# A layer of two token mixers: norms between blocks placed later, and one half-weight's low part made on chip in place of stored and loaded

## The chip, the cores and the metric

The kernel runs on one core of a Trainium2 chip. The metric is the device time of one execution in microseconds, the median over runs. The output is float32, and every large product is made of three products of float32 halves (below).

## The reference

2112 tokens (a prompt of 2048 and a decode of 64) pass one layer of width 1024. All weights are dense matrices.

```python
def encoder_layer(x, p, conv_hist, S0, lb, w_in, conv_w, g_pre, g_onorm, w_a_out, w_b_out, w_o,
                  g_post, g_ple, w_ple_gate, w_ple_proj):
    h = rms_norm(x, g_pre)
    proj = jnp.einsum('btd,dn->btn', h, w_in)
    vA, bA, cA, zA, q, f, iv, zB, gA, gB = split_cols(proj)       # ten groups of 1024 columns
    u = cA * vA
    ...
    yA = jnp.einsum('btc,cd->btd', jax.nn.silu(zA) * bA * conv, w_a_out)
    ...
    fg = lb + (1.0 - lb) * jax.nn.sigmoid(f)
    ...
    S_new, o = hgrn2_scan(S0, qq, kk, vv, logf)                   # 8 heads of 128, chunks of 64
    o = o * lax.rsqrt(jnp.mean(o * o, axis=-1, keepdims=True) + EPS)
    yB = jnp.einsum('btc,cd->btd', o * jax.nn.silu(zB), w_b_out)
    merged = jax.nn.sigmoid(gA) * yA + jax.nn.sigmoid(gB) * yB
    out = jnp.einsum('btd,de->bte', merged, w_o)
    x = x + rms_norm(out, g_post)
    gate = jax.nn.sigmoid(jnp.einsum('btd,de->bte', rms_norm(x, g_ple), w_ple_gate))
    x = x + jnp.einsum('btp,pd->btd', p, w_ple_proj) * gate
```

## The kernel before

**Blocks.** The tokens go through the whole layer in three blocks of 768, 704 and 640, one after the other, features on the partitions. The state of the eight heads and the convolution's history are carried from block to block.

**Products.** A float32 operand is split in a high part `hi` (a copy to the type that TensorE multiplies, made by ScalarE) and a low part `lo` (the operand less `hi`, a subtract on VectorE): `split`, line 230 for both. A product is hi·hi + hi·lo + lo·hi, the matmuls of lines 459, 460 and 461 (the third multiplies the weight's `lo`). The big matrices are taken in pairs of column blocks `i1`, `i2` of 128, each with two halves of its 1024 rows, as 2x2 blocks A11, A12 (both of `i1`), A21, A22 (both of `i2`), and `sgroup` forms their product with seven block products instead of eight (`PRODUCTS`): four of them use sums of weight blocks (S1 to S4), the others A11, A12 and A22. A12 stands fifth. One product is 12 matmuls.

**Where a low part comes from.** In block 0 `combined` loads the weights, makes the sums and splits all; what is asked for later is stored: sums by `keep_sum` (`S<-s`, line 341) and low parts by `split_w` (`low<-lo`, line 288), both on the sync engine's queue SP. In blocks 1 and 2 `kept_w` loads a weight block (`raw`) and makes `hi`; its `lo` is either loaded from the store (`lo<-low`, line 282) or made again on chip (line 230). `used_later(idx, part)` decides in block 0 which low parts are stored, and `among(idx, part)` in `kept_w` which are made on chip. Part 1 is the second half of the rows: A12 for `i1`, A22 for `i2`. The ten groups of columns have the numbers VA, BA, CA, ZA, QQ, FF, IV, ZB, GA, GB from 0 to 9, of eight column blocks each. A head takes its F and Q columns as one pair (`i1` from FF, `i2` from QQ) and its Z and V columns as another (`i1` from ZB, `i2` from IV).

**Order.** Instructions are written by Python generators, and a scheduler that keeps to each engine's written order where it can, with buffers taken from pools (48 row buffers `r`, 4 `lo`, 5 `raw`, 3 `s`), sets the final order. After each product `sgroup` calls `hook()`, which takes the next entry from a list and runs it: so side work is put between products. `spread_out((gen, counts))` fills that list: the n-th number says how many steps of the generator are run after the n-th product from there. `placed` and `paced` bind an instruction or a DMA behind the last matmul written.

**Heads.** Per head `head_prep` makes f, q, k, v with their decays (a scan L986 and L988, exponentials L999 and L1000 on ScalarE, L1002 and L1003 on VectorE); k is turned to rows by tokens (L1072 on VectorE, two DMAs through DRAM, `tk<-r` and `r<-tk`, and a copy L1085 on GpSimd). `head_attn` has TensorE form each chunk's update (L1149), VectorE add it to the state in a chain (L1164, five of them one after the other in block 2), and TensorE multiply the scores (L1187) and the states before (L1189) into the output. Line 1226 scales the head's output, L479 and L488 take products out of the accumulators.

**Norms between blocks.** At the end of block 0 and of block 1, `final_norm` runs among the first gate products of the next block. Its steps: square sums (`sum_squares`, line 749), the first transposes on TensorE that turn the sums to columns (line 726), the root on GpSimd (706), the spread back over the columns by TensorE (714), then a step for each of eight features tiles, a second round of transposes and spread, and a step for each column tile that splits it for the gate (line 230). The x rows are stored and loaded on GpSimd's queue by the same steps. `final_gate` (matmuls of lines 648 to 650) follows after seven products.

Of the kernel before, what the change touches and what calls it, by code (L numbers as in the profile page):

```python
# [20 lines left out]
KB = D // P  # L21
# [10 lines left out]
VA, BA, CA, ZA, QQ, FF, IV, ZB, GA, GB = range(10)  # L32
# [62 lines left out]
def hybrid_step(  # L95
# [46 lines left out]
    def sized(bl, steps):  # L142

        while True:
            with sized_to(bl):
                try:
                    made = next(steps)
                except StopIteration:
                    return
            yield made  # L150
# [4 lines left out]
    def rt(n=0, dt=F32):  # L155
        t = ring.tile([P, BN + 2], dt, tag="r", name=nm("r"))
        return t if n is None else t[:, : n or width[0]]
# [80 lines left out]
    def load_raw(src):  # L238
        raw = wp.tile([P, 4, P], F32, tag="raw", name=nm("raw"), bufs=5)
        SP.dma_start(raw, src)  # L240
        return raw
# [13 lines left out]
    def used_later(idx, part):  # L255

        if idx // 8 in (QQ, IV) and part == 1:
            return False  # L260
        if GA * 8 <= idx < GB * 8 + KB - 2:
            return part in ("S1", "S2", "S3", "S4")
        if idx in (GB * 8 + KB - 1, IV * 8):
            return part != 0
        if idx < QQ * 8:
            return part != 1
        if W_B <= idx < W_O:
            return part == 1 and idx - W_B >= KH
        return True

    def split_w(raw, key=None, spread=False, among_sums=False):


        hi = wp.tile([P, 4, P], F32R, tag="hi", name=nm("hi"))
        if spread:
            lo = low_tile()
            split(raw, hi, lo)
            return hi, lo
        if key in lows:
            lo = wp.tile([P, 4, P], F32R, tag="lo", name=nm("lo")) if among_sums else low_tile()  # L280
            A.copy(hi, raw)  # L281
            SP.dma_start(lo.bitcast(F32), lows[key])
            return hi, lo
        lo = wp.tile([P, 4, P], F32R, tag="lo", name=nm("lo"))
        split(raw, hi, lo)
        if key is not None and used_later(*key):
            lows[key] = dram.tile([P, 4, P], F32, tag=f"lo{key}", name=nm("low"), bufs=1)
            stores[0].dma_start(lows[key], lo.bitcast(F32))
        return hi, lo
# [24 lines left out]
    def behind_all(marks):  # L314

        order = ExitStack()
        for ins in marks:
            order.enter_context(tc.issue_after(ins))
        return order
# [8 lines left out]
    def run(gen, n=None):  # L328
        for i, _ in enumerate(gen):
            if n is not None and i + 1 == n:  # L330
                break
# [12 lines left out]
    def kept_w(i1, i2, name, anew=False, spread=False):  # L344

        def among(idx, part):
            return part == 1 and (idx < QQ * 8 or idx // 8 in (QQ, IV))

        keys = dict(A11=(i1, 0), A12=(i1, 1), A22=(i2, 1))
        if name in keys:  # L350
            return split_w(load_raw(w_blk[keys[name]]), None if anew else keys[name], spread or among(*keys[name]))
        return split_w(load_raw(sums[i1][name]), (i1, name))
# [139 lines left out]
    def half(t, h):  # L492
        return t[:, h * hn() : (h + 1) * hn()]
# [58 lines left out]
    def narrow(src):  # L552
        one = rt(dt=F32R)
        split(src, half(one, 0), half(one, 1))
        return half(one, 0), half(one, 1)
# [979 lines left out]
    def spread_out(*plans):  # L1535


        def steps(todo):
            with behind_all(m for m in copies + adds if m is not None):
                for gen, n in todo:  # L1540
                    run(gen, n)

        for counts in zip_longest(*(plan for _, plan in plans), fillvalue=0):
            todo = [(gen, n) for (gen, _), n in zip(plans, counts) if n]
            hooks.append(partial(steps, todo) if todo else None)
# [131 lines left out]
    for bi, bl in enumerate(blocks):  # L1677
        first, kept = bi == 0, kepts[bi]
        width[0] = bl["n"]
        segs = bl["segs"]  # L1680
        if bi == 1:
            stores[0] = G
        ahead_of = (*range(W_A, W_A + KH), W_O, W_O + 1) if first else None if bl["last"] else range(W_B, W_B + KH)
        path_b(bl, hc, first, kept, fills, hs if first else None, ahead_of and prepare_sums(ahead_of, pieces=True))
        if not bl["last"]:
            run(fills)
        a = []
        nxt = None if bl["last"] else blocks[bi + 1]
        cols, a_first = [], []
        rows = sized(nxt, row_rstd(nxt, cols)) if nxt else iter(())  # L1690
        sums_ahead = prepare_sums((W_O + 2, W_O + 3), True) if first else iter(())

        def side(rows):
            for j in range(KB):
                if 1 <= j <= 5:
                    next(rows, None)
                if j == 2:
                    next(fills, None)
                yield

        def ready():
            a_first.extend(narrow(half(t, 0)) for t in a[:KH])

        path_a(bl, hc, a, first, side(rows), ready)
        assert not hooks
        mg, xo, h2, acc = [], [], [], rt()

        def next_ops():

            with sized_to(nxt):  # L1710
                made = sized(nxt, operands(hc, x_rs[0], partial(load_x, nxt)))
                next(made)
            return made

        def ask_rs():
            with sized_to(nxt):
                x_rs.append(broadcast(cols[0]))

        x_rs = []

        if nxt:
            hc = new_operands()
        stages = [out_in_turn(mg, xo, acc, bl["last"])]
        before, loads, ob, m = merge_in_turn(a, kept, mg, first)
        loads(W_A, -1)
        if first:
            for idx, n in in_turn(before, a_first):
                loads(idx, n)
            next(sums_ahead)
            a_first.clear()  # L1730
            for j, _ in enumerate(merge_plain(bl, ob, m, kept, mg, sums_ahead)):
                if j == KB - 4:
                    ask_rs()
                if j == KB - 2:
                    a_first.extend(narrow(half(t, 0)) for t in mg[:KH])
                    ops = next_ops()
            spread_out((ops, (0, 1, 0, 1, 0, 1, 0) * KH))
            loads = lambda idx, n: None
        else:
            stages = before + stages  # L1740
        if bl["last"]:
            ps = load_p(bl, G)
        for idx, n in in_turn(stages, a_first):
            loads(idx, n)
            if nxt and (idx, n) == (W_B, 4):
                ask_rs()
            elif nxt and (idx, n) == (W_B, 6):
                spread_out((next_ops(), (0, 1, 0, 1, 0, 1, 0) * KH))
            elif nxt:
                pass  # L1750
            elif (idx, n) == (W_B, 5):
                ph = [split_rt(raw) for raw in ps]
            elif (idx, n) == (W_O, 4):
                norms = [final_norm(bl, [s], xo, acc, h2, None, s is segs[1]) for s in segs]
                spread_out((norms[0], (1, 0, 1, 1, 1, 0, 1, 0)))
        if nxt:
            xo.extend(stages[-1]["mid"])
            fills = sized(nxt, gates(nxt, hc, kepts[bi + 1], False))
            norm = sized(bl, final_norm(bl, segs, xo, acc, h2, kept))
            spread_out((norm, (1, 1, 1, 1, 1, 1, 0, 1, 0, 0, 0, 0, 1, 1) + (0, 1) * (KB - 1) + (0, 0, 1, 0, 0, 1) + (0, 1) * (KB - 1) + (1,)))  # L1760
            run(fills, LEAD)
            assert not hooks
            run(final_gate(bl, segs, xo, h2, kept))
        else:

            gate = [final_gate(bl, [s], xo, h2, kept, anew=s is segs[1], held={} if s is segs[1] else {0: 0, 1: 0, 2: 0, 3: 2, 4: 0, 5: 4}) for s in segs]
            spread_out((norms[0], (2, 2, 1, 0, 1, 1, 4, 4)), (norms[1], (0,) * 6 + (1, 1) + (1, 1, 1, 0, 0, 1, 0, 1, 4, 4)))
            run(ple(bl, ph, kept, spare=range(KB)))
            run(gate[0], 2)
            with behind_all(copies[:1]):  # L1770
                run(norms[1], KB)
            run(gate[0])
            assert not hooks
            run(gate[1])
# [49 lines left out]
```

## Time and profile before

| | |
|---|---|
| median of 3 runs | 2522.61 us (2521.67 to 2523.67) |
| the profiled execution's own time | 2521.4 us |
| its span | 2519.7 us |
| granted TensorE clock | 1.0 |
| TensorE busy | 2500.6 us |
| VectorE busy | 1868.3 us |
| ScalarE busy | 1489.6 us |
| GpSimd busy | 480.7 us |
| DMA | 748.77 MB, mean 297 GB/s |
| loads `lo<-low` on SP | 387 of 256 KB |
| stores `low<-lo` on SP | 223 of 256 KB |

The span runs from the first to the last instruction of the profiled execution; the time of a run has some 1.7 us more around it. A busy share is the time in which an engine has an instruction under way. In a timeline a row begins with the start and the length of an instruction in us from the span's start; a bracket at its end is the engine's idle time ahead of it, and what ended it. `x24` is a count, 128x512 a tile of 128 partitions by 512 elements.

### The profile page before, as it was taken

The numbers are of one execution on the slowest core, as the hardware profiler recorded it, in microseconds if no ns is written. First come the engines' busy times: TensorE is split into PE (matmuls) and PEld (weight loads), VectorE is DVE, ScalarE is ACT, GpSimd is POOL, SyncE is SP. The second block draws the span as 40 slices with busy tenths as digits, with TensorE's granted clock in tenths as the row PEclk, the third lists the DMA queues.
The fourth block names the chain that finished last, engine by engine and source line by source line (L and its number), as shares of the span: only waits on it lengthen the run. The fifth ranks groups of instructions, "written<-read, shape, count | busy, mean of one in ns | idle before, by whom it ended". The sixth has DMA issues, their size and how long they took to land.

```text
span 2519.7 us, 47327 instructions
## 1 busy us (share of the span) xinstructions
PE 2500.6 (99%) x16302; PEld 2481.2 (98%) x16302; DVE 1868.3 (74%) x3607; ACT 1489.6 (59%) x2902; POOL 480.7 (19%) x819
## 2 busy tenths in 40 slices
PE   9999999999999999999999999999999999999999
PEld 9999999999999999999999999999999999999998
DVE  7888898988868775577785657987357776446967
ACT  6666676654453764466655556576456665545675
POOL 2032223221022021122223211102212221001111
PEclk9999999999999999999999999999999999999999
DMA  8788988997697798788889988979988997878985
GB/s 333 250 300 316 333 323 303 348 328 270 231 348 244 244 332 299 266 285 302 303 289 315 346 297 301 331 266 333 327 292 308 313 303 262 266 255 313 338 272 200
DMA packets 350961, 748.77 MB, mean 297 GB/s; under 512 B 43702, under 2 KB 49136, under 8 KB 350720
## 3 DMA queue, kind: packets, MB, share of 16 engines
q1 hardware_dynamic: 298944, 541.26, 62.3%
q0 software_dynamic: 51776, 204.48, 23.1%
q8 instruction: 128, 2.10, 0.3%
q14 instruction: 113, 0.93, 0.1%
HBM read 540.29 MB, written 205.28 MB: 296 GB/s over the span
## 4 chain that ended last, share of the span: by engine, by line
PE 88%; DVE 4%; DMA 3%; issue 3%; ACT 1%; POOL 0%; SPq 0%; DVEq 0%; ACTq 0%; POOLq 0%
PE pg L459 19%; PE pg L461 19%; PE pg L460 18%; PE pg L611 5%; PE pg L610 5%; PE pg L612 5%; PE pg L650 3%; PE pg L649 3%; PE pg L648 3%; DMA raw<-w_blk 1%; PE pa L1117 1%; PE pa L1187 1%; PE pa L1149 1%; PE pa L1189 1%; DVE lo L230 1%
## 5 line engine op out<-in xcount | busy, mean ns | idle before, releaser
L459 PE MATMUL pg<-r,hi 128*128 128x320 f32 (+2 forms) x3304 | 1074.9, 325 | 1.9 <-ACT hf L473 1.2
L460 PE MATMUL pg<-r,hi 128*128 128x320 f32 (+2 forms) x3304 | 1067.1, 323 | 0.0
L461 PE MATMUL pg<-r,lo 128*128 128x384 f32 (+2 forms) x2380 | 776.2, 326 | 3.3 <-DVE lo L230 3.0
L281 ACT CAST hi<-raw 128x512 fp32r<-128x512 f32 x626 | 386.4, 620 | 434.2 <-PE pg L460 188.9
L459 PEld LDWEIGHTS pg<-r,hi 128*128 128x128 f32 x3304 | 621.2, 188 | 4.7 <-ACT hf L473 1.9
L460 PEld LDWEIGHTS pg<-r,hi 128*128 128x128 f32 x3304 | 621.3, 188 | 0.0
L461 PEld LDWEIGHTS pg<-r,lo 128*128 128x128 f32 x2380 | 447.1, 188 | 5.4 <-DVE lo L230 4.2
L230 ACT CAST hi<-raw 128x512 fp32r<-128x512 f32 x348 | 215.6, 622 | 181.1 <-PE pg L460 48.2
L461 PE MATMUL pg<-r,s 128*128 128x352 f32 (+1 forms) x924 | 292.0, 316 | 0.0
L611 PE MATMUL pg<-r,hi 128*128 128x320 f32 (+2 forms) x864 | 277.6, 322 | 0.9 <-DVE r L230 0.8
L610 PE MATMUL pg<-r,hi 128*128 128x320 f32 (+2 forms) x864 | 274.9, 322 | 0.0
L230 DVE TENSOR_TENSOR r<-r,r 128x320 fp32r<-128x320 f32 (+7 forms) x350 | 206.4, 608 | 45.0 <-ACT r L230 43.2
L230 DVE TENSOR_TENSOR lo<-raw,hi 128x512 fp32r<-128x512 f32 x264 | 181.1, 689 | 76.6 <-ACT hi L230 71.7
L230 ACT CAST r<-r 128x320 fp32r<-128x320 f32 (+7 forms) x350 | 183.8, 556 | 45.8 <-DVE r L403 11.9
L612 PE MATMUL pg<-r,lo 128*128 128x352 f32 (+2 forms) x564 | 180.7, 321 | 0.0
L461 PEld LDWEIGHTS pg<-r,s 128*128 128x128 f32 x924 | 173.4, 188 | 0.0
L230 ACT CAST hi<-s 128x512 fp32r<-128x512 f32 x164 | 101.7, 623 | 115.4 <-PE pg L460 87.5
L649 PE MATMUL pg<-r,hi 128*128 128x384 f32 (+2 forms) x512 | 166.9, 327 | 0.2 <-DVE r L230 0.2
L648 PE MATMUL pg<-r,hi 128*128 128x384 f32 (+2 forms) x512 | 165.8, 327 | 0.2 <-ACT hi L281 0.2
L611 PEld LDWEIGHTS pg<-r,hi 128*128 128x128 f32 x864 | 162.1, 188 | 2.8 <-DVE r L230 2.2
L610 PEld LDWEIGHTS pg<-r,hi 128*128 128x128 f32 x864 | 161.3, 188 | 1.3 <-ACT r L230 0.7
L473 ACT COPY hf<-pg 128x352 f32<-128x352 f32 (+2 forms) x354 | 157.0, 447 | 1.1 <-PE pg L461 1.1
(383 smaller groups left out, 4155.3 us busy)
## 6 DMA issues: line engine op xcount, KB each, us to landing
raw<-w_blk SPq DMA_DIRECT2D x579, 256.0 KB, 4.4
raw<-S SPq DMA_DIRECT2D x436, 256.0 KB, 4.2
lo<-low SPq DMA_DIRECT2D x387, 256.0 KB, 4.3
s<-low SPq DMA_DIRECT2D x239, 256.0 KB, 4.5
low<-lo SPq DMA_DIRECT2D x223, 256.0 KB, 4.0
S<-s SPq DMA_DIRECT2D x152, 256.0 KB, 3.9
low<-r POOLq DMA_DIRECT2D x50, 256.0 KB, 4.7
r<-w_blk POOLq DMA_DIRECT2D x48, 256.0 KB, 6.6
```

Source lines behind the costliest of these rows:

```text
L230: return A.copy(hi, src).ins, V.tensor_tensor(lo, src, hi.bitcast(F32), ALU.subtract).ins
L281: A.copy(hi, raw)
L459: add(hi[:, k, :], xhi, start=start and k == 0, stop=False)
L460: add(hi[:, k, :], xlo, start=False, stop=False)
L461: last[0] = add(lo[:, k, :], xhi, start=False, stop=k == KH - 1).ins
L473: copied = A.copy(got[n], ps[bank])
L610: add(hi[:, k, :], xhi, start=start and k == 0, stop=False)
L611: add(hi[:, k, :], xlo, start=False, stop=False)
L612: last[0] = add(lo[:, k, :], xhi, start=False, stop=k == KH - 1).ins
L648: T.matmul(ps, hi[:, k % 4, :], xhi[:, c], start=k == ks[0], stop=False)
L649: T.matmul(ps, hi[:, k % 4, :], xlo[:, c], start=False, stop=False)
L650: last[0] = T.matmul(ps, lo[:, k % 4, :], xhi[:, c], start=False, stop=k == ks[-1]).ins
```

## The change

Two edits. The first: the second half-rows' low parts of the F and Z groups (A12 of both pairs of every head) are no longer stored in block 0 nor loaded in blocks 1 and 2, but made on chip by a subtract. The Q and V groups' A22 was already so; the A12 of the first four groups too. 16 stores and 32 loads go, 32 subtracts come. The second: the list of counts for the norms between blocks. Counted in products from 0, the first transposes move from 7 to 11, their spread from 12 to 14, the eight column steps from 13, 15, ... 27 to 15, 17, ... 29, the second transposes from 30 to 32, the second spread from 33 to 35, and the last steps from 35, 37, ... 47, 48 to 36, 38, 40, 42, 44, 46, 47, 48.

```diff
-        if idx // 8 in (QQ, IV) and part == 1:
-            return False
         if GA * 8 <= idx < GB * 8 + KB - 2:
             return part in ("S1", "S2", "S3", "S4")
         if idx in (GB * 8 + KB - 1, IV * 8):
-            return part != 0
-        if idx < QQ * 8:
+            return part != 0 and (part != 1 or idx >= GA * 8)
+        if idx < GA * 8:
             return part != 1
...
     def kept_w(i1, i2, name, anew=False, spread=False):
         def among(idx, part):
-            return part == 1 and (idx < QQ * 8 or idx // 8 in (QQ, IV))
+            return part == 1 and idx < GA * 8
...
-            spread_out((norm, (1, 1, 1, 1, 1, 1, 0, 1, 0, 0, 0, 0, 1, 1) + (0, 1) * (KB - 1) + (0, 0, 1, 0, 0, 1) + (0, 1) * (KB - 1) + (1,)))
+            spread_out((norm, (1,) * 6 + (0,) * 5 + (1, 0, 0, 1, 1) + (0, 1) * (KB - 1) + (0, 0, 1, 0, 0, 1) + (1, 0) * (KB - 3) + (1, 1, 1)))
```

The two removed lines stand at the top of `used_later`, so that from there on every line of the changed kernel has a number two lower: its L1162 is L1164 of before. The numbers behind tile names count up in the order of allocation.

The sync engine's queue in block 0, in the first heads, before: between two loads of weights stand a store of a sum (L341) and stores of low parts (L288).

```order
L341 DMA S_646_2709<-s_2707 128x512
L288 DMA low_2506<-lo_2503 128x512
L240 DMA raw_2699<-w_blk 128x512
L240 DMA raw_2930<-w_blk 128x512
L341 DMA S_651_2719<-s_2717 128x512
L288 DMA low_2512<-lo_2509 128x512
L240 DMA raw_2932<-w_blk 128x512
L288 DMA low_2526<-lo_2523 128x512
L341 DMA S_656_2729<-s_2727 128x512
```

The same place of that queue after the change (the stores of sums are L339, of low parts L286 there):

```order
L339 DMA S_639_2695<-s_2693 128x512
L286 DMA low_2494<-lo_2491 128x512
L240 DMA raw_2685<-w_blk 128x512
L240 DMA raw_2914<-w_blk 128x512
L339 DMA S_644_2705<-s_2703 128x512
L240 DMA raw_2916<-w_blk 128x512
L286 DMA low_2512<-lo_2509 128x512
L339 DMA S_649_2715<-s_2713 128x512
```

One of the two stores of low parts between the last two sums is gone (A12's); the rest of the order, and that of the other engines in block 0, is the same.

VectorE in a head of block 2, before: the scan (L986, L988), the five steps of the state's chain (L1164, the first with `state`, the last into `one`) and what stands between them.

```order
L986 SCALAR_TENSOR_TENSOR r_24350<-keep,r_24349 128x640
L1164 SCALAR_TENSOR_TENSOR r_24442<-state_14315,qc_23954,pa_24437 128x128
L988 TENSOR_TENSOR r_24349<-r_24350 128x640
L230 TENSOR_TENSOR s_24398<-raw_24395,hi_24397 128x512
L1164 SCALAR_TENSOR_TENSOR r_24442<-r_24442,qc_23954,pa_24437 128x128
L1226 TENSOR_TENSOR r_23555<-r_24103,r_23555 128x640
L1164 SCALAR_TENSOR_TENSOR r_24442<-r_24442,qc_23954,pa_24437 128x128
L1003 COPY qc_24360<-qc_24360 128x1
L488 TENSOR_TENSOR hf_24435<-hf_24435,hf_24467 128x320
L1164 SCALAR_TENSOR_TENSOR r_24442<-r_24442,qc_23954,pa_24437 128x128
L1002 TENSOR_TENSOR qc_24360<-qc_24360,r_24351 128x9
L479 TENSOR_TENSOR hf_24420<-hf_24420,pg_24486 128x320
```

The same head after the change, each line number two lower:

```order
L984 SCALAR_TENSOR_TENSOR r_24318<-keep,r_24317 128x640
L230 TENSOR_TENSOR lo_24360<-raw_24357,hi_24359 128x512
L230 TENSOR_TENSOR s_24366<-raw_24363,hi_24365 128x512
L986 TENSOR_TENSOR r_24317<-r_24318 128x640
L1162 SCALAR_TENSOR_TENSOR r_24410<-state_14283,qc_23922,pa_24405 128x128
L1224 TENSOR_TENSOR r_23523<-r_24071,r_23523 128x640
L1162 SCALAR_TENSOR_TENSOR r_24410<-r_24410,qc_23922,pa_24405 128x128
L1001 COPY qc_24328<-qc_24328 128x1
L1000 TENSOR_TENSOR qc_24328<-qc_24328,r_24319 128x9
L1162 SCALAR_TENSOR_TENSOR r_24410<-r_24410,qc_23922,pa_24405 128x128
L477 TENSOR_TENSOR hf_24388<-hf_24388,pg_24454 128x320
L1162 SCALAR_TENSOR_TENSOR r_24410<-r_24410,qc_23922,pa_24405 128x128
```

The new subtract (`lo` from `raw`) and the old one (into an `s` buffer) stand ahead of the chain's first step, and L1002 (L1000 there) ahead of its third.

TensorE where the norm between blocks 0 and 1 makes its first transposes (L726), before:

```order
L459 MATMUL pg_11193<-r_10855,hi_11120 128x352
L460 MATMUL pg_11193<-r_10856,hi_11120 128x352
L461 MATMUL pg_11193<-r_10855,lo_11121 128x352
L726 MATMUL pa_11164<-ident,r_8743 128x128 x3
L726 MATMUL pa_11169<-ident,r_8743 128x128 x3
L459 MATMUL pg_11148<-r_10323,hi_11132 128x352
```

And after the change:

```order
L457 MATMUL pg_11116<-r_10869,hi_11100 128x352
L458 MATMUL pg_11116<-r_10870,hi_11100 128x352
L459 MATMUL pg_11116<-r_10869,lo_11101 128x352
L724 MATMUL pa_11189<-ident,r_8711 128x128 x3
L724 MATMUL pa_11194<-ident,r_8711 128x128 x3
L457 MATMUL pg_11131<-r_10239,hi_11106 128x352
```

The product that came next before (`pg_11148`, called `pg_11116` after) and the one behind it now stand ahead of the transposes: they are 24 matmuls later. At the boundary of blocks 1 and 2 they are 16 matmuls later.

## The prediction

> **What bounds the kernel now.** I read the page first: the span, the share of each engine, the chain that ended last.
> ```profile
> span 2519.7 us, 47327 instructions
> PE 2500.6 (99%) x16302; PEld 2481.2 (98%) x16302; DVE 1868.3 (74%) x3607; ACT 1489.6 (59%) x2902; POOL 480.7 (19%) x819
> PE 88%; DVE 4%; DMA 3%; issue 3%; ACT 1%; POOL 0%; SPq 0%; DVEq 0%; ACTq 0%; POOLq 0%
> ```
> TensorE is busy for 99% of the span, and the chain is 88% TensorE. The change takes no matmul away, so it can only win or lose the gaps between matmuls. Next I asked for TensorE's waits in the stretches that the change touches: the heads of block 0 (100 to 460 us), the norms between blocks (870 to 960 and 1690 to 1790) and the heads of block 1 (1040 to 1330).
> ```profile
> PE pg L461 <- DVE lo L230: 3.0, 2, 1.7
> PE pg L459 <- ACT hf L473: 1.2, 2, 0.7
> PE pg L459 <- ACT hi L230: 0.6, 1, 0.6
> ...
> PE pa L726 <- DVE r L749: 1.2, 1, 1.2
> ...
> PE pa L726 <- DVE r L749: 1.4, 1, 1.4
> PE pa L714 <- POOL cols L706: 0.2, 1, 0.2
> ...
> PE pa L1149 <- POOL r L1085: 0.4, 1, 0.4
> ```
> The first three rows are block 0's: 4.8 us, and a fourth row of 0.2 us makes 5.0. The next three are the boundaries', the last is block 1's only one. The heads of block 2 (1790 to 2130) have no TensorE wait at all. So 5.0 + 2.8 + 0.4 us is nearly all that can be won there, and nothing hinders block 2 today: what the change adds there can only cost.
>
> The waits of VectorE over block 0's heads (100 to 460) say why TensorE waits for `lo`:
> ```profile
> DVE lo L230 <- DMA low<-lo: 19.8, 10, 4.4
> ```
> It stands still ten times until a store of a `lo` tile has landed, because the buffer that it wants to write is still being read by that store.
>
> **The change part by part.**
>
> *Stores that go (block 0).* 16 of the `low<-lo` stores go, those of A12 in the eight F and eight Z groups. The timeline shows one of them issued on the sync queue, three of the waits it is part of, and a TensorE stall soon after:
> ```profile
> 155.76 0.69 DVE L230 TENSOR_TENSOR lo<-s,hi 128x512 fp32r<-128x512 f32 x1 [3.29 <-DMA low<-lo]
> ...
> 199.74 1.97 SPq L288 DMA_DIRECT2D low<-lo  x1
> ...
> 208.75 0.69 DVE L230 TENSOR_TENSOR lo<-s,hi 128x512 fp32r<-128x512 f32 x1 [4.38 <-DMA low<-lo]
> ...
> 220.15 0.44 PE L461 MATMUL pg<-r,lo 128*128 128x384 f32 x1 [1.71 <-DVE lo L230]
> ...
> 408.20 0.69 DVE L230 TENSOR_TENSOR lo<-s,hi 128x512 fp32r<-128x512 f32 x1 [3.66 <-DMA low<-lo]
> ```
> The bracket is the idle time ahead of the instruction and what ended it. Matched with the program's order, the five longest of the ten waits (first and last quoted, the longest between) are all waits for A12's stores; they go, and that is most of the 19.8 us. TensorE's stall at 220.15 comes 11 us after VectorE was held for 4.38 us, with its split of the next weights late. If VectorE is no longer held, all 5.0 us of TensorE's idle time go: −5.0. The bounds are −6 (each of six stalls also refills the pipeline, about 0.16 us each) and −2 (the stores of sums that stay are next in the queue, and only the two stalls at `lo` shorten). I take −5.0. The splits themselves are unchanged in block 0.
>
> *Norms.* The columns' sums must be transposed by TensorE when VectorE has the last square sum ready. These rows show the stall:
> ```profile
> 888.05 0.32 PE L460 MATMUL pg<-r,hi 128*128 128x352 f32 x1
> 888.21 0.32 PE L461 MATMUL pg<-r,lo 128*128 128x352 f32 x1
> 889.72 0.44 PE L726 MATMUL pa<-ident,r 128*128 128x128 f32 x2 [1.18 <-DVE r L749]
> ```
> Matmuls start 0.16 us apart, so the 24 matmuls by which the first transposes move at this boundary are 24 x 0.16 = 3.8 us, and the 16 at the other 2.6 us: more than the 1.18 and 1.4 us of the waits. They go, and with them a third of 0.2 us at the second boundary, where the spread waits for the column's root; each saves a refill of 0.16 too: 1.2 + 1.4 + 0.2 + 3 x 0.16 = 3.3 us. What is late next is the end of the norm: the whole chain runs 24 matmuls later, and its last columns are put closer.
> ```profile
> 970.00 0.95 DVE L230 TENSOR_TENSOR r<-r,r 128x768 fp32r<-128x768 f32 x1
> ...
> 971.59 0.34 PE L649 MATMUL pg<-r,hi 128*128 128x384 f32 x1
> ```
> The last column's low half is done at 970.95, and the matmul that opens the gate product with it starts at 971.59: 0.64 us of slack. With two columns now one slot closer, that slack can go; the x stores on GpSimd's queue that hang on the same steps come in a bunch, with the gate's x loads behind them. I price the end at +0.8, between 0 and +1.8 (one more stall like the 1.4 us one, with its refill, at one boundary, and 0.2 at the other). Norms: −2.5.
>
> *The low half made on chip (blocks 1 and 2).* 32 loads of 256 KB leave the sync queue, 32 subtracts go on VectorE, 16 a block, two a head. VectorE has room on the whole (74% busy), but not at one place in each head. In block 2 one of the two stands, with another split of sums and the second half of a scan behind it, ahead of the state's chain (five instructions L1164), and L1002 comes ahead of the third of them. One head of before:
> ```profile
> 1944.41 0.32 DVE L1164 SCALAR_TENSOR_TENSOR r<-state,qc,pa 128x128 f32<-128x128 f32 x1
> ...
> 1945.38 0.69 DVE L230 TENSOR_TENSOR s<-raw,hi 128x512 fp32r<-128x512 f32 x1
> 1945.98 0.34 DVE L1164 SCALAR_TENSOR_TENSOR r<-r,qc,pa 128x128 f32<-128x128 f32 x1
> ...
> 1946.98 0.34 DVE L1164 SCALAR_TENSOR_TENSOR r<-r,qc,pa 128x128 f32<-128x128 f32 x1
> 1947.89 0.15 DVE L1003 COPY qc<-qc 128x1 f32<-128x1 f32 x1 [0.57 <-ACT qc L999]
> ...
> 1948.36 0.34 DVE L1164 SCALAR_TENSOR_TENSOR r<-r,qc,pa 128x128 f32<-128x128 f32 x1
> 1948.62 0.17 DVE L1002 TENSOR_TENSOR qc<-qc,r 128x9 f32<-128x9 f32 x1
> 1948.70 0.48 DVE L479 TENSOR_TENSOR hf<-hf,pg 128x320 f32<-128x320 f32 x1
> 1949.10 0.34 DVE L1164 SCALAR_TENSOR_TENSOR one<-r,qc,pa 128x128 f32<-128x128 f32 x1
> ...
> 1947.76 0.72 ACT L1000 ACTIVATE r<-r 128x640 f32<-128x640 f32 x1
> ...
> 1948.65 0.39 PE L1189 MATMUL pa<-r,r 128*128 128x128 f32 x2
> 1948.87 0.39 PE L1187 MATMUL pa<-r,att 128*128 128x128 f32 x2
> ...
> 2066.31 0.39 PE L1187 MATMUL pa<-r,att 128*128 128x128 f32 x2
> ```
> L1187 reads the fourth state, done at 1948.70: slack 0.17 us. Now the new order, with starts from these rows. From 1944.41 to 1946.98 run two L1164, a scan half, a split and L1226, 2.57 us without a gap; with one more subtract (0.60 from start to start) the same work ends at 1947.58. L1003 still waits for ScalarE until 1947.89. L1002 then waits for ScalarE's L1000, done at 1947.76 + 0.72 = 1948.48, so it starts at about 1948.52; the third L1164 at 1948.60 (before at 1946.98), L479 at 1948.86, the fourth L1164 at 1949.26, done at 1949.60. TensorE, which came at 1948.87, starts at about 1949.64: +0.77 us. Matched wait by wait with the program, six heads, 29.36 us apart, the last with its L1187 at 2066.31, have this slack of 0.17; one before them has 1.8 and I give it 0.2: 6 x 0.77 + 0.2 = +4.8 us. The bounds are 0 (ScalarE, held by the same matmuls, does L1000 earlier against the shifted head) and +5.5 (all seven whole). What was queued behind the wait of L1002 on VectorE are exactly the third and the fourth state, and TensorE waits for them; that is why the price is near the upper end.
>
> In block 1 the same kind of subtract lands behind the state's chain but in a loop: TensorE's L1149, the states, VectorE's transposes of k, two DMAs, GpSimd's copy L1085, the next head's L1149.
> ```profile
> 1219.55 0.82 POOL L1085 COPY r<-r 128x768 f32<-128x768 f32 x1 [7.68 <-DMA r<-tk]
> 1220.43 0.38 PE L1149 MATMUL pa<-r,r 128*128 128x128 f32 x1 [0.41 <-POOL r L1085]
> ...
> 1251.36 0.82 POOL L1085 COPY r<-r 128x768 f32<-128x768 f32 x1 [7.16 <-DMA r<-tk]
> ...
> 1252.83 0.49 PE L1149 MATMUL pa<-r,r 128*128 128x128 f32 x3
> ```
> One loop from 1220.43 to the copy's end at 1252.18 is 31.75 us, TensorE's own head 32.40, so a subtract of 0.60 just fits into 0.65. The two DMAs of some 7 us gain from 32 fewer loads in the queues (an estimate of 0.3 to 0.6). I take +0.2: two heads stall a little more, the one that stalls now may stop. Bounds −0.6 and +2.
>
> *A rule weighed.* Two instructions of before lie over one another:
> ```profile
> 2078.82 0.68 DVE L230 TENSOR_TENSOR s<-raw,hi 128x512 fp32r<-128x512 f32 x1
> ...
> 2078.88 1.59 POOL L1085 COPY r<-r 128x640 f32<-128x640 f32 x1 [2.77 <-DMA r<-tk]
> ```
> The copy that takes 0.82 us alone at a larger size takes 1.59 here: 0.77 more, about one split's length. The Trainium skill's page "SBUF — State Buffer", section "Who interferes with whom", says that a VectorE instruction with two SBUF inputs contends with a GpSimd instruction that reads SBUF, and that the later one is blocked fully. By that rule each of the 32 new subtracts is a new chance to hold L1085, which speaks against the change; the trace agrees at 2078.88. In the sum I count it at nothing, since VectorE's new subtracts stand at another time of the head than the copy; it is the third rival's price.
>
> *Sum.* −5.0 − 2.5 + 0.2 + 4.8 = −2.5 us. The profiled execution took 2521.4 us around its span of 2519.7, 1.2 below the median of 2522.6: 2521.4 becomes 2518.9, the median **2520.1**. About 0.2%, 5.05 us, is what a measurement of this kernel can tell from no change; −2.5 is within it.
>
> **The rivals.**
>
> *Block 2 doesn't stall.* The 0.77 us hangs on ScalarE's L1000 and on 0.17 us of slack, in a head that repeats; if ScalarE runs 0.6 us further ahead, L1002 doesn't wait. For it: today ScalarE is ahead of VectorE by little, and only L999 was waited for. Against: L1000 follows L999 directly. Then −7.3 us: 2515.3, faster. Chance 0.20.
>
> *Block 0's wait is replaced.* The sums' stores, three per pair of groups, stay on the same queue, and VectorE's next waits are for weights. Only the stalls at `lo` shorten, −2 in place of −5: with block 2's price −2.5 + 3.0 = +0.5, 2523.1, no change. Chance 0.10.
>
> *Block 1's loop becomes the bound.* The subtract adds 0.60 to the loop and, if the shift lays L1085 over a split as at 2078.88, 0.77 more: 1.37 against a slack of 0.65 is 0.72 a head, over seven returns +5.0. It takes the place of the +0.2: −2.5 − 0.2 + 5.0 = +2.3, 2524.9, slower than before. It decides from a loop lengthened by 0.65 us on, and passes 0.2% at 1.75 us. For it: one head of block 1 stalls already. Against: the copy stood alone in both rows of block 1 quoted. Chance 0.10.
>
> **How the numbers follow.** My forecast holds with 0.60, its own range 2517.3 to 2523.4: block 0 between −6 and −2, the norms' end from 0 to +1.8, block 2 from +3 to +5.5. The range reaches to both outer rivals: 2515.0 to 2525.0. Faster by over 0.2% (below 2517.6): most of the first rival, 0.17, and 0.06 of the forecast, 0.23. Slower by over 0.2% (above 2527.7): half of the third rival and a little of a norm's end gone wrong, 0.07. Within: 0.70.
>
> **What would show it.** In block 0, VectorE's wait for `low<-lo` falls from 19.8 to about 4 us and TensorE's 5.0 us go to under 1. At the boundaries L726 has no wait for L749; there may be one at the gate's last column. In block 2's heads, TensorE's waits, none before, are six of about 0.6 to 0.8 us at L1189 or L1187 for L1164, with L1002 waiting for L1000 on VectorE. In block 1, the time from L1149 to L1149 stays under 32.5 us. I am wrong if block 2 shows no such wait (faster), or if L1149 waits for L1085 in most heads (slower).

## The result, and the profile after

The changed kernel takes 2516.85 us, median of 14 runs (2514.02 to 2520.05), beside 2521.97 us of the kernel before in 14 runs: ratio 0.9982, 95% interval 0.9975 to 0.9990, or 2.5 to 6.3 us less. The forecast was 2520.1 us, a gain of 2.5 us, in a range from 2515.0 to 2525.0. The profiled executions are 4.7 us apart (2521.4 and 2516.69 us).

The page of the changed kernel; its line numbers are two lower than those of before:

```profile
span 2515.0 us, 47257 instructions
PE 2500.4 (99%) x16302; PEld 2481.1 (99%) x16302; DVE 1887.6 (75%) x3639; ACT 1491.5 (59%) x2902; POOL 481.0 (19%) x819
PE 92%; DVE 3%; DMA 2%; ACT 1%; issue 1%; POOL 0%; SPq 0%; ACTq 0%; DVEq 0%; POOLq 0%
```

TensorE's work is the same, and its share of the chain that ended last is 92% in place of 88%. VectorE is 19.3 us busier: 32 subtracts of 0.60 us from start to start. To see where the time went, I put the start of the same TensorE instruction (the n-th recorded, 16302 in both) side by side and took the difference by stretches of the kernel before, in us:

```
stretch of before (us)               before    after   step the prediction had
0-100     first products              98.94    -0.93   -
100-460   heads of block 0           359.97    -7.27   -5.0 (-6 to -2)
460-870   rest of block 0              410.00    +0.00   -
870-1040  norms, blocks 0 to 1       169.96    -0.38   )
1690-1860 norms, blocks 1 to 2       170.06    -1.91   ) -2.5
1040-1690 block 1                    650.00    +1.87   +0.2 (-0.6 to +2)
1860-2110 heads of block 2           250.03    +4.97   +4.8 (0 to +5.5)
2110-2515 the rest of block 2        404.77    -1.02   -
```

What the change doesn't touch (the first and the last row, −0.93 and −1.02) shows how far such a row can be off in one execution: about 1 us; in e1_norms below, block 1's heads, which its edit leaves alone, are 1.45 us off. A row is one execution of each kernel, so one that comes back in several kernels counts for more.

TensorE's waits in the same stretches as before. 100 to 460 has no row any more, and 1040 to 1330 one:

```profile
PE pg L457 <- DVE r L505: 1.0, 1, 1.0
...
PE pa L1147 <- POOL r L1083: 1.2, 1, 1.2
...
PE pg L457 <- DVE r L505: 0.7, 1, 0.7
...
PE pa L1185 <- DVE r L1162: 1.0, 6, 0.2
PE pa L1187 <- DVE r L1162: 1.0, 5, 0.2
```

First and third row are the boundaries: the wait for the square sums (L749) is gone, and another stands in its place, for the adds L507 (here L505). On VectorE these adds stand behind the last square sums (here L747) and one split:

```profile
879.34 2.02 DVE L747 TENSOR_TENSOR r<-r,r 128x768 f32<-128x768 f32 x2 [0.40 <-ACT r L746]
881.28 0.68 DVE L230 TENSOR_TENSOR s<-raw,hi 128x512 fp32r<-128x512 f32 x1
881.88 0.51 DVE L505 TENSOR_TENSOR r<-hf,pg 128x352 f32<-128x352 f32 x1
```

Of the waits above, the second (at L1147) is in block 1's heads, and the last two in the heads of block 2, where before there was no wait. VectorE's waits in block 0's heads:

```profile
DVE lo L230 <- ACT hi L230: 16.3, 22, 1.4
DVE lo L230 <- DMA low<-lo: 3.4, 3, 1.4
```

The wait for stores fell from 19.8 to 3.4 us; in its place VectorE waits longer for ScalarE, 16.3 us where it was 7.6, and TensorE waits for neither in this stretch.

A head of block 2 after the change, VectorE's rows first, then TensorE's:

```profile
1936.74 0.67 DVE L230 TENSOR_TENSOR lo<-raw,hi 128x512 fp32r<-128x512 f32 x1
...
1940.20 0.15 DVE L1001 COPY qc<-qc 128x1 f32<-128x1 f32 x1 [0.20 <-ACT qc L997]
1940.82 0.17 DVE L1000 TENSOR_TENSOR qc<-qc,r 128x9 f32<-128x9 f32 x1 [0.47 <-ACT r L998]
1940.91 0.34 DVE L1162 SCALAR_TENSOR_TENSOR r<-r,qc,pa 128x128 f32<-128x128 f32 x1
...
1941.57 0.34 DVE L1162 SCALAR_TENSOR_TENSOR r<-r,qc,pa 128x128 f32<-128x128 f32 x1
...
1941.31 0.49 PE L1187 MATMUL pa<-r,r 128*128 128x128 f32 x2 [0.19 <-DVE r L1162]
1941.96 0.49 PE L1185 MATMUL pa<-r,att 128*128 128x128 f32 x2 [0.17 <-DVE r L1162]
```

The added subtract, then the wait of L1002 (here L1000) for ScalarE's exponential, then the third and fourth state: the chain that the prediction wrote down, and TensorE waits twice a head. The two brackets say 0.36 us, but the head is 0.80 us longer. Before, these matmuls start 0.11 us apart, while each is recorded as some 0.28 us long, so they overlap. Idle time is counted from the recorded end of the matmul ahead: at a bracket of 0.19 us the start is 0.35 us later than before, and the next start another 0.10.

### The profile page after: what moved, and what is told of

Read it like the earlier page. It is cut to its first block, busy times and chain, and to the rows that moved or that the text cites. A ratio compares the mean times of both kernels' runs of the same rounds, so it can differ in the third digit from the quotient of the medians.

```text
span 2515.0 us, 47257 instructions
## 1 busy us (share of the span) xinstructions
PE 2500.4 (99%) x16302; PEld 2481.1 (99%) x16302; DVE 1887.6 (75%) x3639; ACT 1491.5 (59%) x2902; POOL 481.0 (19%) x819
## 4 chain that ended last, share of the span: by engine, by line
PE 92%; DVE 3%; DMA 2%; ACT 1%; issue 1%; POOL 0%; SPq 0%; ACTq 0%; DVEq 0%; POOLq 0%
PE pg L457 20%; PE pg L458 20%; PE pg L459 20%; PE pg L609 5%; PE pg L608 5%; PE pg L610 5%; PE pg L648 3%; PE pg L647 3%; PE pg L646 3%; PE pa L1147 1%; PE pa L1115 1%; PE pa L1185 1%; PE pa L1187 1%; DMA raw<-w_blk 1%; PE pa L1318 0%
## 5 line engine op out<-in xcount | busy, mean ns | idle before, releaser
L230 DVE TENSOR_TENSOR lo<-raw,hi 128x512 fp32r<-128x512 f32 x296 | 202.4, 686 | 79.8 <-ACT hi L230 78.0
```

The lines of the kernel that those rows point to most:

```text
L230: return A.copy(hi, src).ins, V.tensor_tensor(lo, src, hi.bitcast(F32), ALU.subtract).ins
```

## The experiments

All start from the kernel before or the changed one, and have the line numbers of the kernel before. Where a stretch is compared, it is the table's, in the profiled execution.

**The norms alone (e1_norms)**: the list of counts of the change, low parts as before.

```diff
-            spread_out((norm, (1, 1, 1, 1, 1, 1, 0, 1, 0, 0, 0, 0, 1, 1) + ...
+            spread_out((norm, (1,) * 6 + (0,) * 5 + (1, 0, 0, 1, 1) + ...
```

> The kernel before with the new list of counts for the norms alone; low parts stored and loaded as before. My theory: the plan trades TensorE's waits for the square sums (L749) for a shorter wait for the adds L507 that stand behind the same square sums on VectorE, so the two boundaries give about -2.0 us together (-0.4 and -1.7), block 0's heads, block 1's and block 2's heads stay as before (5.0, 0.4 and 0 us of TensorE waits): about 2.0 us less than the kernel before. Rival: the wait for L507 and the better second boundary come from the changed traffic of low parts, not from the plan; then the boundaries give -3.3 us with no wait for L507, or nothing at the second one.

Measured: 2519.56 us beside 2522.33, ratio 0.9990 (0.9982 to 0.9999). This is 2.8 us less than the kernel before, and its profiled execution (2516.63 us) is another 2.9 below its own median, so its rows flatter it. The boundaries' stretches give −1.01 and −2.90 us, block 0's heads −0.49 and block 2's −0.63. TensorE's wait at the first boundary and its longest in block 0's heads, then VectorE's wait for stores there:

```profile
PE pg L459 <- DVE r L507: 0.4, 1, 0.4
...
PE pg L461 <- DVE lo L230: 2.1, 2, 1.7
```
```profile
DVE lo L230 <- DMA low<-lo: 22.2, 10, 4.2
```

The wait for L507 comes with the plan, as my theory had it, and block 0's waits are the old ones. The wait is only 0.4 us here and absent at the second boundary, where the changed kernel has 1.0 and 0.7; the plan alone gains more at the boundaries (3.9 us) than inside the changed kernel (2.3). So the rival, by which the traffic of low parts has a share in this wait, isn't excluded.

**The low parts alone (e2_low)**: `used_later` and `among` as changed, counts as before.

```diff
-            return part == 1 and (idx < QQ * 8 or idx // 8 in (QQ, IV))
+            return part == 1 and idx < GA * 8
```

> The other edit alone: A12's low parts of the F and Z groups made on chip, not stored and not loaded; the norms' counts as before. My theory: block 0 gives -7 us, block 1's heads lose 1 to 2 us to the loop through the copy L1085, block 2's heads lose 5.0 us at L1187 and L1189, the waits at the boundaries are those of the kernel before (1.2 and 1.6 us): in all -0.5 to -1.5 us. Rival: block 0's gain is an accident of the run and not of the edit; then the kernel is 4 to 6 us slower than before.

Measured: 2517.41 us beside 2522.33, ratio 0.9978 (0.9969 to 0.9986). Block 0's heads −7.27, block 2's +4.84, the boundaries as before. TensorE's waits at the two boundaries and in block 2's heads:

```profile
PE pa L726 <- DVE r L749: 0.9, 1, 0.9
...
PE pa L726 <- DVE r L749: 1.1, 1, 1.1
...
PE pa L1189 <- DVE r L1164: 1.1, 6, 0.2
PE pa L1187 <- DVE r L1164: 1.0, 6, 0.2
```

Each edit makes its own waits. In all it is 4.9 us faster than the kernel before, where I had expected 0.5 to 1.5: block 1's heads did not lose 1 to 2 us but gained 0.91.

**The stores put back (e3_stores)**: the changed kernel with `used_later` of before.

```diff
+        if idx // 8 in (QQ, IV) and part == 1:
+            return False
...
-            return part != 0 and (part != 1 or idx >= GA * 8)
-        if idx < GA * 8:
+            return part != 0
+        if idx < QQ * 8:
```

> The changed kernel, but block 0 still stores the 16 low parts of A12 (nobody reads them later): what it does in blocks 1 and 2 is as in the changed kernel. If the stores' hold on the lo buffers was what cost TensorE its waits in block 0, the whole gain there (7 us) goes, VectorE's wait for low<-lo is back at about 20 us, and the kernel is about 2 us slower than the kernel before and 7 slower than the changed one. Rival: the gain in block 0 has another source; then it stays within 2 us of the changed kernel.

Measured: 2524.35 us beside 2522.33, ratio 1.0008 (1.0000 to 1.0017), 7.5 us above the changed kernel's median. Block 0's heads are +0.92 instead of −7.27. VectorE's and TensorE's wait there:

```profile
DVE lo L230 <- DMA low<-lo: 23.4, 9, 3.9
```
```profile
PE pg L461 <- DVE lo L230: 2.7, 2, 1.7
```

So the gain in block 0 is the 16 stores, and what follows from them: nobody reads what they write, and still they cost 8 us of TensorE's time. VectorE's wait for their landing comes back with them, which fits the hold on the buffers of `lo`. Their place on the sync queue, ahead of loads, came back too, and no run with more `lo` buffers tells the two apart.

**The chain cleared of L1002 (e4_order)**: the changed kernel with L1002 and L1003 of block 2 behind the state's chain.

```diff
-            V.tensor_tensor(f[:, 1:nch], r[:, 1:nch], ...)
-            V.tensor_copy(f[:, 0:1], r[:, 0:1])
+            with behind_all(chained if bl["last"] and hd else ()):
+                V.tensor_tensor(f[:, 1:nch], r[:, 1:nch], ...)
+                V.tensor_copy(f[:, 0:1], r[:, 0:1])
...
-                V.scalar_tensor_tensor(ss[:, i, :], cur, ...)
+                chained[0] = V.scalar_tensor_tensor(ss[:, i, :], cur, ...).ins
```

> The changed kernel, with L1002 and L1003 of block 2's heads held behind the state's chain (the five L1164) in VectorE's order; the added subtract stays ahead of the chain. My theory: L1002's wait for ScalarE's L1000 inside the chain costs most of the 0.8 us per head, so TensorE's waits for L1164 fall from 2.0 us in 11 to under 0.8 us, a head is 29.4 to 29.6 us long in place of 30.2, and the kernel is 3 to 5 us faster than the changed one. Rival: the added subtract itself (0.6 us ahead of the chain) is the price; then the waits stay at 1.5 us or more and less than 2 us is gained.

Measured: 2511.81 us beside 2522.33, ratio 0.9959 (0.9946 to 0.9972). Block 2's heads are +0.98 in place of +4.97, and the waits for L1164 are below what the view lists. The same head as above:

```profile
1936.45 0.66 DVE L230 TENSOR_TENSOR lo<-raw,hi 128x512 fp32r<-128x512 f32 x1
...
1940.02 0.34 DVE L1164 SCALAR_TENSOR_TENSOR r<-r,qc,pa 128x128 f32<-128x128 f32 x1
...
1940.68 0.34 DVE L1164 SCALAR_TENSOR_TENSOR r<-r,qc,pa 128x128 f32<-128x128 f32 x1
...
1941.98 0.17 DVE L1002 TENSOR_TENSOR qc<-qc,r 128x9 f32<-128x9 f32 x1
...
1941.07 0.49 PE L1187 MATMUL pa<-r,att 128*128 128x128 f32 x2
```

The subtract still stands ahead of the chain; the fourth state starts at 4.23 us behind it, in the changed kernel at 4.83. The stretch is 3.99 us shorter than in the changed kernel, some 0.66 for each of the six heads that lost 0.80: that was the wait put into the chain, and the rest, about 1 us over the stretch, stays with the subtract or is within what a row can be off.

**The square sums later (e5_sums)**: as e4_order, and the last step of sums and the loads of x two products later.

```diff
-(1,) * 6 + (0,) * 5 + (1, 0, 0, 1, 1)
+(1, 1, 1, 0, 0, 1, 1, 1, 0, 0, 0, 1, 0, 0, 1, 1)
```

> As e4_order, and in the norms' list of counts the last step of square sums and the two steps that load x stand two products later ((1, 1, 1, 0, 0, 1, 1, 1, 0, ...) in place of six ones in a row), so that VectorE does the adds L507 ahead of the last two L749; the transposes stay at count 11. My theory: the waits for L507 at the two boundaries (1.4 and 1.3 us in e4_order) are the square sums queued ahead of them; they go, L726 doesn't wait either (it had some 3.8 us of room), and the boundaries' two stretches are 2 to 3 us shorter than e4_order's. Rival: the sums are now late for the transposes; then L726 waits for L749 again, by 1 us or more, and nothing is gained.

Measured: 2513.88 us beside 2521.75, ratio 0.9970 (0.9960 to 0.9980), not faster than e4_order (its median is 2.1 us higher, and the intervals overlap). TensorE's waits for L507 in e4_order at the two boundaries first, then the waits of e5_sums at the first (one row) and the second (two):

```profile
PE pg L459 <- DVE r L507: 1.4, 1, 1.4
...
PE pg L459 <- DVE r L507: 1.3, 1, 1.3
```
```profile
PE pg L461 <- DMA lo<-low: 0.9, 1, 0.9
...
PE pg L461 <- DMA lo<-low: 1.1, 1, 1.1
PE pa L726 <- DVE r L749: 0.5, 1, 0.5
```

The waits for L507 are gone at both, so they were the sums queued ahead of the adds. The first boundary (870 to 1040) gains 1.2 us on e4_order, a wait of 0.9 for a load at its end counted in. At the second, a wait of 1.1 us for a load of a low part and 0.5 at L726 give all back.

**Only the F groups on chip (e6_f_only)**: Z's A12 stored and loaded as before the change.

```diff
-        if idx < GA * 8:
+        if idx < ZB * 8:
...
-            return part == 1 and idx < GA * 8
+            return part == 1 and idx < ZB * 8
```

> The changed kernel, but only the F groups' A12 is made on chip; the Z groups' A12 is stored in block 0 and loaded in blocks 1 and 2 as before the change (8 stores and 16 loads more than the changed kernel). My theory: five of the six A12 stores that VectorE waited for in block 0 are F's, so block 0 keeps 5 to 7 of its 7.3 us; the subtract that delays the state's chain in block 2 is Z's, so block 2's heads lose nothing (0 to 0.5 us in place of 5.0). In all 3 to 5 us faster than the changed kernel. Rival: each store counts alike and each subtract too; then half of block 0's gain and half of block 2's loss are left, and the kernel is within 1.5 us of the changed one.

Measured: 2511.76 us beside 2521.75, ratio 0.9962 (0.9948 to 0.9976). Block 0's heads keep −6.44 of the −7.27, block 2's heads are −0.30 with no TensorE wait. VectorE's wait for stores in block 0, and TensorE's one wait there:

```profile
DVE lo L230 <- DMA low<-lo: 3.5, 5, 1.5
```
```profile
PE pa L1149 <- POOL r L1085: 0.6, 1, 0.6
```

That one wait is for the copy L1085, at 354 us, and it is the whole 0.83 us that block 0 lacks here. e9_f_only_sums below stores the same low parts, has no such wait, and its row is −7.27. So F's stores carry all of block 0's gain. Two halves of one edit with opposite signs: F's stores were the ones in the way, and Z's subtract is the one that hurts (Z alone was not run).

**Block 2 at block 1's slots (e7_slots)**: the changed kernel, `head_attn` two products earlier in block 2.

```diff
-                at(6 + late, *attn)
-                at(8 + late, *attn)
+                at(6, *attn)
+                at(8, *attn)
```

> The changed kernel, with block 2's two steps of head_attn at the slots of block 1 (6 and 8 in place of 8 and 10): L1149, the state's chain and L1187, L1189 come 24 matmuls (3.5 us) earlier in each head, the chain ahead of the added subtract. My theory: block 2's 5.0 us go, since L1149 had 5.8 us or more of room behind the copy L1085 in seven heads and 3.1 in one; 4 to 5 us faster than the changed kernel. Rival: the loop through L1085 that binds block 1 binds block 2 as well, L1149 waits for L1085 in most heads, and the kernel is no faster than the changed one.

Measured: 2511.03 us beside 2521.75, ratio 0.9962 (0.9950 to 0.9975). Block 2's heads −0.20 us, with no wait: the chain is over before the added subtract starts.

```profile
1933.08 1.07 DVE L1164 SCALAR_TENSOR_TENSOR r<-r,qc,pa 128x128 f32<-128x128 f32 x3
1934.26 0.35 DVE L1164 SCALAR_TENSOR_TENSOR one<-r,qc,pa 128x128 f32<-128x128 f32 x1
...
1936.64 0.67 DVE L230 TENSOR_TENSOR lo<-raw,hi 128x512 fp32r<-128x512 f32 x1
```

**The repairs together (e8_slots_sums, e9_f_only_sums)**: e5_sums's counts on e7_slots and on e6_f_only.

> e7_slots and e5_sums' list of counts together, on the changed kernel: block 2's heads at block 1's slots, and the last square sums behind the adds L507. If the two repairs are independent, block 2 keeps its 5 us, the first boundary's wait for L507 (0.9 us and its refill in e7_slots) goes, the second boundary loses its 1.2 us but for a rest of 0.5 at L726: 1 to 2.5 us faster than e7_slots. Rival: loads of x come later with the sums and delay the columns; then it is no faster than e7_slots.

> e6_f_only with e5_sums' list of counts: the F groups' A12 alone on chip, slots of block 2 as before the change, the last square sums behind the adds L507. Expected 0.5 to 2 us faster than e6_f_only (waits for L507 of 0.8 and 0.7 us go, a rest of 0.5 at L726 comes). Rival: as for e8_slots_sums.

Measured: e8_slots_sums 2514.31 us beside 2521.15, ratio 0.9971 (0.9962 to 0.9980), not faster than e7_slots: its median is 3.3 us higher, where 1 to 2.5 lower was expected, and the intervals overlap. The boundaries gain on it (0.3 and 0.8 us), but block 2's heads lose 1.9. About 0.9 of that is one wait for the copy at L1149 and the start behind it, so at the earlier slots L1149 has little room behind the copy; the other 1 us is spread thin, and its cause is open. TensorE's one wait there:

```profile
PE pa L1149 <- POOL r L1085: 0.6, 1, 0.6
```

e9_f_only_sums has the lowest median, 2510.50 us, ratio 0.9960 (0.9947 to 0.9972); from e6_f_only (0.9962) and e4_order (0.9959) it can't be told apart. All three, and e7_slots, beat both kernels: some 10 us below the one before, 5 to 6 below the changed one.

## Why the prediction was right

Its range held the time, and the direction and the main mechanisms came as written, but the gain is about twice the 2.5 us forecast: 5.1 us by medians, 4.5 by the ratio. Whether the likeliest case came depends on the measure: 2516.85 us is below its line for faster by over 0.2% (2517.6, chance 0.23), the ratio's 0.18% is within. The time also lies 0.45 us below the range of its main case, 2517.3 to 2523.4. That range is narrower than the bounds it names for the three steps, which add up to 2516.5 and 2524.8 with block 1 at +0.2. By its steps:

- *Stores that go* (−5.0, bounds −6 to −2): mechanism right, size too small, and outside its bounds. It came to −7.27, and e3_stores, which puts only the stores back, takes 8.2 away. The mis-sized term is the idle time of the wait view, taken for the whole: the prediction counted 0.16 us of refill behind each wait at the norms, and here only in the bound. In the trace of before, seven delays in that stretch are 6.3 us by the excess over the usual pitch of the matmuls, with 5.0 us shown as waits; the instruction behind each is another 0.1 us late, 0.7 in all.
- *The five longest waits are A12's*: e6_f_only bears it out. Five of the six stores that I had matched are F's, and F alone brings 6.4 of 7.3 us in one kernel and all of it in e9_f_only_sums.
- *Norms* (−2.5): −2.3 us, but not by the steps as written. The three waits went, as forecast. The price was set on the end of the norm (the last column, +0.8), and neither boundary has a wait at the gate's last column. What came late next was the adds L507: they stand on VectorE behind the square sums and one split, in the product that waited before too, but TensorE stood still for the sums first. Taking the first of two waits at one queue away uncovered the second. e5_sums and e8_slots_sums, which move the sums behind the adds, have no wait for L507.
- *Block 2* (+4.8): +4.97, +4.84 with this edit alone, +4.96 with the stores back. The sum over rows of the trace of before gave the place, the wait on VectorE and the size. The shape differs: not six waits of 0.6 to 0.8 us, but two of about 0.2 a head, for the third state at L1189 and the fourth at L1187, which with the late starts behind them come to 0.80; e4_order shows the wait for L1000 inside the chain to be the larger part, e6_f_only that Z's subtract is the cause.
- *Block 1* (+0.2): its heads are +0.97 us in the profiled run of the changed kernel, with one wait of 1.2 us at L1149. Three other kernels with both subtracts in block 1's heads (e2_low, e3_stores, e4_order) have −0.91, −0.28 and −0.62 us; e1_norms, which has none of it, +1.45. So this wait is not shown to be the change's; the price is about nothing. The sign given, under 32.5 us from L1149 to L1149, was missed once, with 33.73 us at this wait; the copy ahead of it, at 1276.56, took its usual 0.82 us, and came after 9.30 us of idle time that its DMA ended.
- *The loop's DMAs* (a gain of 0.3 to 0.6 us, an estimate): too low, by these runs. In block 1's heads, `tk<-r` landed 3.3 us after its issue ended before (median of eight) and 2.1 in the changed kernel, 2.1 in e2_low, e3_stores and e4_order, and 3.7 in e1_norms, which keeps the loads; `r<-tk` stayed at 6.7 to 7.1. GpSimd's wait for `tk<-r` fell with it, from 12.7 to 5.6 us. That is some 1.1 us a head, more than the subtract's 0.60. It goes with the loads that left, though no run took the loads away alone.
- *The rivals*: the first (block 2 doesn't stall) is refuted by the 11 waits; the second (block 0's wait replaced) by a stretch without a wait; the third (block 1's loop bound) by the three kernels above.

That the profiles differ by 4.7 us where the forecast was 2.5 comes to two rows that the change doesn't touch (−1.95 us together), −2.27 at block 0, +1.67 at block 1 and +0.4 at the norms and block 2. The misses at blocks 0 and 1 nearly cancel, which is luck.

Two things stay open. The wait for L507 is 0.4 us and none in e1_norms, 1.0 and 0.7 in the changed kernel, 1.4 and 1.3 in e4_order, with the same counts; what else moves it was not tried. And the parts don't add up: −2.8 us (e1_norms) and −4.9 (e2_low) by medians make −7.7, the changed kernel has −5.1; each has an interval of some 2 us to either side, so these 2.6 us may be noise.

## What to carry to other kernels

Where a scheduler keeps an engine full, price an added instruction by what stands behind it on its queue at its place, not by the engine's load: VectorE had a quarter of its time free, and one subtract ahead of a serial chain, with a wait that slid into that chain, cost 5 us in block 2's heads. A store that nobody reads isn't free: 16 of them cost 8 us here, most likely by the buffers that they hold. And take an edit apart by tile: here one half of it gave the gain in block 0 and the other half the loss in block 2, and the first half alone is 5 us better than the whole.

## What the runs showed of the hardware

The Trainium skill's page "SBUF — State Buffer", section "Who interferes with whom", was the rule that the prediction weighed: the later of two contending instructions of VectorE and GpSimd is blocked. The traces show both orders. In block 0 of the changed kernel the copy comes first and keeps its 0.82 us, and the split behind it takes 0.93 in place of 0.69; four other heads of block 0 have the same pair, with splits of 0.92 to 0.93:

```profile
151.02 0.82 POOL L1083 COPY r<-r 128x768 f32<-128x768 f32 x1 [6.32 <-PE pg L459]
```
```profile
151.45 0.93 DVE L230 TENSOR_TENSOR lo<-s,hi 128x512 fp32r<-128x512 f32 x1 [1.42 <-ACT hi L230]
```

In block 2 a copy that starts 0.57 us behind L1034 (here L1032) and runs beside more of VectorE's instructions takes 1.86 us; the group's row (minimum, median and maximum in ns) has 714 for the shortest of its kind:

```profile
1893.44 0.83 DVE L1032 TENSOR_TENSOR r<-r,qc 128x640 f32<-128x640 f32 x1
...
1894.01 1.86 POOL L1083 COPY r<-r 128x640 f32<-128x640 f32 x1 [2.51 <-DMA r<-tk]
```
```profile
L1083 POOL COPY r<-r x24: 714/822/1857, 103.7 to 2078.5; 128x768 f32<-128x768 f32 x16, 128x640 f32<-128x640 f32 x8
```

The split's delay (0.24 us) is less than the 0.39 us for which the copy went on beside it, so "fully blocked" is not what these rows show for a split behind a copy, as far as the profile's rough spans of GpSimd go. The Trainium skill's page has the words "fully blocks" where it speaks of VectorE's 2-port modes; of an instruction with two SBUF inputs it says that it contends, under one rule of an exclusive lock. The prediction's own row, 1.59 us, was set against the 0.82 of a larger copy; against 0.71 at its own size it is 0.88 us more, and beside it run four of VectorE's instructions, so one split's length isn't shown to be the price. TensorE has no wait at the two places shown.

What I had not expected is the price of a short wait: 0.36 us of idle time in two waits made a head 0.80 us longer.
